# Norm scales from one product with ones, and shared landing buffers in the gate/up stage

## The chip, the cores and the metric

The kernel runs as one program on one core of a Trainium2 chip. A core has five engines, each with its own queue of instructions that it works off in order: TensorE (PE, matrix products; its weight loads are listed apart as PEld), VectorE (DVE), ScalarE (ACT), GpSimd (POOL) and SyncE (SP), which here only issues transfers. Engines wait for one another through semaphores. On-chip data lies in SBUF (128 partitions), products land in PSUM banks of 128 x 512 float32, and DMA engines move data between SBUF and device memory. The metric is the device time of one execution in microseconds. Three runs of the kernel before took 3178.4, 3183.67 and 3187.15 us; the median is 3183.67 us.

## The reference, cut to what matters

One layer of a decoder on 2048 positions of width 1024, in float32. The change touches the second norm, the gate/up and down products behind it, and the final norm:

```python
def rms_norm(x, g):
    y = xf * lax.rsqrt(jnp.mean(xf * xf, axis=-1, keepdims=True) + EPS)
    return (y * g).astype(x.dtype)

x = x + merged @ w_out
h = rms_norm(x, norm_ffn)
x = x + (jax.nn.silu(h @ w_gate) * (h @ w_up)) @ w_down
return rms_norm(x, final_norm)
```

`merged` is the gated sum of a sparse attention branch and a gMLP branch; both come earlier in the program and are not touched. D_FF is 2816.

## The kernel before

Activations are kept transposed: features on the partitions, positions along the free dimension, in tiles of 128 x 512. Every large product is made from three products of rounded parts: a float32 operand is split into a high part h (ACT copies it to the reduced type fp32r) and a low part l (DVE subtracts h), and PE sums h*h, h*l and l*h (`split` and `mm3`, lines 149 to 165). So each operand of each product needs an ACT copy and a DVE (or POOL) subtraction before PE can use it.

The program has stages one behind the other. The last three matter here.

**Output projection (1590 to 1883 us of the trace).** For each of four blocks `j` of 512 positions, the attention branch is projected and merged, eight tiles `m` of `merged @ w_out` are made into the PSUM tile `po`, x is added (`xo`), the result goes to device memory (`d_x1`, issued by ACT), and its squares are summed over `m` into `sq3`. When the next block reaches m = 1, `stats` (line 1055) makes the norm scales of the block that is done: PE takes the sums over partitions with four small products with a column of ones (`pss3`, one column for 128 positions), DVE copies four columns, ACT takes the root, DVE the reciprocal, and 512 scales `rr` are written to device memory as a row `d_rr`. `prep_b` (line 1020) then prepares the normed activations of half the positions (two blocks n) for two of the eight feature tiles (k and k + 4): per block it loads the row of scales back, spread over all partitions (`rbf`), loads two tiles of x (`x1s`), multiplies, and makes from the four tiles the seven right-hand operands of a Strassen product (`SB`; five are sums or differences, tile `cmb`, two are tiles as they are). They are written to device memory (`d_b`); in half 0 the operand for i = 1 is split at once and stays on chip. Half 0 is prepared in this stage (four calls, with blocks j = 2 and 3), half 1 in four calls after the pairs 2, 4, 6 and 8 of the gate/up stage.

**Gate/up (1883 to 2743 us).** The loops run over two halves of 1024 positions, eleven pairs `p` of feature tiles, seven Strassen products `i` in the order 1, 4, 5, 7, 3, 2, 6, and gate and up (g and u). Each of the 14 products of a pair has 12 matmuls of 512 columns into a bank `pgu`. Weights come in 1 MB transfers (`fraw`, three buffers); POOL forms their sums (`cmb`), ACT and DVE split them (`wfh`, `wfl`, six buffers each, so the splits run up to six products ahead). Products are copied by ACT and added by DVE into tiles `s`; at the pair's end `store_acts` makes silu(gate) * up, and DVE forms five sums and writes seven tiles to device memory (`d_a`). In pair 0 of half 0, `load_b` fetches the prepared operands one i at a time (`braw`) and splits them into `fh`, `fl`; pair 10 does the same for half 1. All short-lived tiles of this stage (`s`, `cmb` of DVE, `braw`, `rbf`, `x1s`) come from one set of 16 buffers, `tmp` (line 1158), opened when the output projection has closed its pools.

**Down (2743 to 3193 us).** Seven Strassen products over the pairs, with operands fetched from `d_a` and `d_w` and split again (`ua`, `uw`), PSUM tile `pdn`, sums `acc`. When a quarter is complete, `final` makes the final norm: four small products with ones, a DVE copy, root and reciprocal, then `bcast_rows` (line 134), which puts each scale on the diagonal of a 128 x 128 tile, in a high and a low part, and spreads it over the partitions with two products with `onesr`; ACT copies the result out of PSUM, DVE multiplies eight tiles, SP writes them to the output. This happens five times, three times for 512 positions and twice for 256; the last of them ends the program.

The order in which each engine works is not the order of the source. The program is built with a scheduler that simulates it and places each instruction where its model of the time finds room; a pool's buffers decide what can be placed early, since a tile can be written only when the tile that had its buffer is done with.

## Time and profile before

| what | value |
|---|---|
| median of three runs | 3183.67 us |
| the profiled execution, whole | 3195.09 us |
| its span, first to last instruction | 3193.0 us |
| mean granted TensorE clock | 0.978 of 2.4 GHz |
| busy share of the span | PE 96%, DVE 68%, ACT 45%, POOL 36% |
| PE busy, 1590 to 1883 us (output projection) | 278.3 of 293 us, clock 0.98 |
| PE busy, 1883 to 2743 us (gate/up) | 847.1 of 860 us, clock 0.99 |
| PE busy, 2743 to 3177 us (down) | 428.6 of 434 us, clock 1.00 |

The profiled execution is 11.4 us (0.4%) longer than the median run, so differences worked out from it are set against its own time and then carried over to the median. A busy share says how long an engine had an instruction in it. The granted clock says how much of the full 2.4 GHz TensorE was given: it has two levels, 1.2 and 2.4 GHz, so a stretch with a mean of 0.83 was in part at the lower one. A wait in the profile is put down to the engine or transfer whose signal came last.

### The profile page before, as it was taken

What the parts mean: (1) busy time and instruction counts of PE and PEld (TensorE: products, weight loads), DVE (VectorE), ACT (ScalarE), POOL (GpSimd) and SP (SyncE); (2) the same over time, 40 slices, a digit from 0 to 9 for tenths busy, and PEclk for the clock granted to TensorE, in tenths of its full rate; (3) what the DMA queues carried; (4) which work ended last, traced back from release to release, by engine and by line L of the source; (5) the groups of instructions that cost most, each with busy time, mean ns of one, the idle gap of its engine ahead of it and who ended that gap; (6) DMA issues with size and microseconds to landing.
All of it is one profiled execution on the core that took longest, in us unless ns stands there. A gap on an engine that the chain in (4) does not pass through costs nothing.

```text
span 3193.0 us, 43147 instructions
## 1 busy us (share of the span) xinstructions
PE 3057.4 (96%) x14550; PEld 2528.5 (79%) x14550; DVE 2162.7 (68%) x3846; ACT 1450.4 (45%) x2720; POOL 1163.4 (36%) x1186
## 2 busy tenths in 40 slices
PE   8799999999899999999899989999999999999998
PEld 7677888778688787888777778888878888788887
DVE  5648769869544787788643647777876777544565
ACT  6444554454234676677521134333443334333442
POOL 4453232343232323233353323333345555521220
PEclk9899999999899999999999999999999999999999
DMA  6533343333553222222465853444544444854453
GB/s 198 174 124 126 109 130 105 128 130 109 180 173 124 77 71 82 70 77 65 149 200 152 287 160 113 159 148 142 201 172 167 169 159 162 284 174 139 138 189 106
DMA packets 275681, 464.89 MB, mean 146 GB/s; under 512 B 41473, under 2 KB 99330, under 8 KB 275330
## 3 DMA queue, kind: packets, MB, share of 16 engines
q1 hardware_dynamic: 254146, 399.19, 39.3%
q0 software_dynamic: 16704, 54.54, 4.6%
q10 hardware_dynamic: 4608, 8.39, 0.7%
q8 instruction: 114, 1.87, 0.3%
q14 instruction: 109, 0.89, 0.1%
HBM read 307.93 MB, written 154.09 MB: 145 GB/s over the span
## 4 chain that ended last, share of the span: by engine, by line
PE 58%; DVE 6%; DMA 6%; ACT 2%; issue 2%; POOL 0%; SPq 0%; DVEq 0%; ACTq 0%; POOLq 0%
PE pgu L164 8%; PE pgu L163 8%; PE pgu L165 8%; PE pdn L164 4%; PE pdn L163 4%; PE pdn L165 4%; PE ptp L870 3%; DVE Pt L853 2%; PE O L877 2%; PE O L878 2%; PE ppr L163 1%; PE ppr L165 1%; PE ppr L164 1%; PE pg L165 1%; PE pg L163 1%
## 5 line engine op out<-in xcount | busy, mean ns | idle before, releaser
L1010 POOL TENSOR_TENSOR cmb<-fraw 128x512 f32<-128x512 f32 x275 | 401.5, 1465 | 487.4 <-DVE wfl L156 424.9
L163 PE MATMUL pgu<-fh,wfh 128*128 128x512 f32 x1232 | 480.2, 391 | 9.5 <-ACT fh L155 5.8
L164 PE MATMUL pgu<-fl,wfh 128*128 128x512 f32 x1232 | 481.9, 391 | 2.7 <-DVE fl L156 2.7
L165 PE MATMUL pgu<-fh,wfl 128*128 128x512 f32 x1232 | 481.5, 391 | 0.8 <-DVE wfl L156 0.7
L163 PEld LDWEIGHTS pgu<-fh,wfh 128*128 128x128 f32 x1232 | 232.4, 189 | 60.2 <-ACT fh L155 7.0
L164 PEld LDWEIGHTS pgu<-fl,wfh 128*128 128x128 f32 x1232 | 232.8, 189 | 52.4 <-DVE fl L156 4.0
L165 PEld LDWEIGHTS pgu<-fh,wfl 128*128 128x128 f32 x1232 | 232.7, 189 | 50.4 <-DVE wfl L156 2.4
L497 DVE SCALAR_TENSOR_TENSOR X<-rl,wi,X 128x512 f32<-128x512 f32 (+3 forms) x266 | 217.3, 820 | 78.6 <-ACT rl L493 63.1
L155 ACT ACTIVATE wfh<-cmb 128x512 fp32r<-128x512 f32 x220 | 138.5, 630 | 280.9 <-POOL cmb L1010 158.5
L156 DVE TENSOR_TENSOR wfl<-cmb,wfh 128x512 fp32r<-128x512 f32 x220 | 193.4, 886 | 101.2 <-ACT wfh L155 100.8
L164 PE MATMUL pdn<-ua,uw 128*128 128x512 f32 (+1 forms) x660 | 247.8, 376 | 3.9 <-DVE ua L156 3.9
L165 PE MATMUL pdn<-ua,uw 128*128 128x512 f32 (+1 forms) x660 | 245.9, 376 | 0.0
L163 PE MATMUL pdn<-ua,uw 128*128 128x512 f32 (+1 forms) x660 | 239.7, 376 | 1.5 <-ACT ua L155 1.5
L156 DVE TENSOR_TENSOR ua<-raw,ua 128x512 fp32r<-128x512 f32 (+1 forms) x165 | 121.0, 737 | 176.1 <-ACT ua L155 176.0
L1184 DVE TENSOR_TENSOR s<-s,pgu 128x512 f32<-128x512 f32 x264 | 174.7, 680 | 77.2 <-PE pgu L165 40.5
L163 PE MATMUL pm<-wh,hT 128*128 128x512 f32 (+1 forms) x576 | 218.7, 387 | 6.4 <-ACT wh L155 5.6
L164 PE MATMUL pm<-wl,hT 128*128 128x512 f32 (+1 forms) x576 | 219.5, 383 | 0.3 <-POOL wl L156 0.2
L155 ACT ACTIVATE pth<-ptp 128x512 fp32r<-128x512 f32 (+1 forms) x320 | 162.5, 532 | 123.9 <-PE ptp L870 114.6
L165 PE MATMUL pm<-wh,lT 128*128 128x512 f32 (+1 forms) x576 | 218.6, 381 | 0.0
L493 ACT ACTIVATE rl<-sc 128x512 f32<-128x512 f32 (+3 forms) x304 | 155.5, 547 | 133.2 <-PE sc L491 111.0
L163 PE MATMUL pg<-hT,wh 128*128 128x512 f32 x512 | 201.9, 394 | 8.0 <-ACT zg L458 8.0
L155 ACT ACTIVATE ua<-raw 128x512 fp32r<-128x512 f32 (+1 forms) x165 | 99.0, 602 | 242.4 <-PE pdn L165 204.2
(301 smaller groups left out, 7511.9 us busy)
## 6 DMA issues: line engine op xcount, KB each, us to landing
raw<-d_a SPq DMA_DIRECT2D x143, 256.0 KB, 2.7
wraw<-in_w_in_dram SPq DMA_DIRECT2D x64, 512.0 KB, 4.2
d_a<-cmb SPq DMA_DIRECT2D x110, 256.0 KB, 2.3
fraw<-in_w_gate_dram SPq DMA_DIRECT2D x22, 1024.0 KB, 5.1
fraw<-in_w_up_dram SPq DMA_DIRECT2D x22, 1024.0 KB, 6.8
d_sg<-zg POOLq DMA_DIRECT2D x64, 256.0 KB, 3.1
sg<-d_sg SPq DMA_DIRECT2D x64, 256.0 KB, 3.4
d_w<-cmb SPq DMA_DIRECT2D x55, 256.0 KB, 2.2
```

What stands on the lines that cost most here:

```text
L155: act.activation(h, src, AF.Copy)
L156: lo.tensor_tensor(l, src, _f(h), op=ALU.subtract)
L163: pe.matmul(out, ah, bh, start=first, stop=False, skip_group_check=onto)
L164: pe.matmul(out, ah, bl, start=False, stop=False, skip_group_check=onto)
L165: pe.matmul(out, al, bh, start=False, stop=last, skip_group_check=onto)
L493: act.activation(r[:, :w], sc[:, :w], AF.Relu)
L497: dve.scalar_tensor_tensor(xs, r[:, :w], wi[:, i, h:h + 1], xs, op0=ALU.mult, op1=ALU.add)
L853: dve.tensor_tensor_reduce(tiles[-1][0][:, po:po + w], sc[:, :w], masks[i][:, c0:c0 + w], -0.125, big if last is None else last, ALU.add, ...
L870: pe.transpose(pt[:, t * P:(t + 1) * P], out["P"][t, kt // 8][:, (kt % 8) * P:(kt % 8 + 1) * P], ident)
L877: pe.matmul(O[:, cs], V, a[:, cs], start=(kt == 0), stop=False)
L1010: eng.tensor_tensor(s, blocks[form[0]], blocks[form[1]], op=form[2])
L1184: dve.tensor_tensor(s[to], s[to], b, op=op)
```

## The change

The scales of both norms come from one product. `rms_rows` multiplies a 128 x 128 tile of ones with the tile of summed squares, in float32, so every partition holds the sum of every position; ACT takes the root from PSUM over the whole tile, and DVE the reciprocal of the whole tile. `stats` and `final` use it; `bcast_rows`, `onesr` and the row `d_rr` are gone. The scales of half 0 stay on chip in two buffers (`rbs`) until the last `prep_b` of half 0 has read them; those of half 1 are written as a full tile to `d_rb` and loaded from there.

The pool `pb` that held the short-lived tiles of `prep_b` in the output projection stays open through the gate/up stage: it has the two scale tiles and five buffers `pb3` instead of seven. `load_b`, `prep_b` of half 1 and the five sums of `store_acts` take these five buffers; only the sums of the very last pair take `tmp`, which has 12 buffers instead of 16.

```diff
--- before.py
+++ after.py
@@ -77,7 +77,7 @@
-    d_rr = tc.dram_tile([S], F32, name="d_rr")
+    d_rb = tc.dram_tile([P, S], F32, name="d_rb")
...
-    def bcast_rows(dst, cols, ntile, mk, tag):
-
-        for t0 in range(0, ntile, 4):
-            n = min(4, ntile - t0)
-            w = slice(0, n * P)
-            dh, dl = mk()
-            for t in range(n):
-                ts_, c = slice(t * P, (t + 1) * P), cols[:, t0 + t:t0 + t + 1]
-                dve.tensor_scalar(dh[:, ts_], ident, c, None, op0=ALU.mult)
-                dve.scalar_tensor_tensor(dl[:, ts_], ident, c, _f(dh[:, ts_]), op0=ALU.mult, op1=ALU.subtract)
-            pb = bank(tag, "pbc")
-            pe.matmul(pb[:, w], onesr, dh[:, w], start=True, stop=False)
-            pe.matmul(pb[:, w], onesr, dl[:, w], start=False, stop=True)
-            act.activation(dst[:, t0 * P:(t0 + n) * P], pb[:, w], AF.Copy)
+    def rms_rows(dst, sq, pb, sd):
+
+        pe.matmul(pb, ones, sq, start=True, stop=True)
+        act.activation(sd, pb, AF.Sqrt, bias=eps6, scale=1.0 / D)
+        dve.reciprocal(dst, sd)
...
-    pb_, _ = open_pool("pb", side="right", stack=c3)
+    pb_, _ = open_pool("pb", side="right", stack=c34)
...
-            rb = mk("rbf")
-            sp.dma_start(rb, d_rr[rows].partition_broadcast(P))
+            if half:
+                rb = mk("rbf")
+                sp.dma_start(rb, d_rb[:, rows])
+            else:
+                rb = rbs[n]
...
-        return pb_.tile([P, 512], dt, name=name, tag="pb3", bufs=7)
-
-    def stats(sa, rows, pl, tag="C"):
-
-        pss = bank(tag, "pss3")
-        for t in range(4):
-            pe.matmul(pss[:, t:t + 1], sa[:, t * P:(t + 1) * P], ones[:, 0:1], start=(t == 0), stop=(t == 3))
-        ss = pl.tile([P, 4], F32, name="ss3")
-        dve.tensor_copy(ss, pss[:, 0:4])
-        rr = pl.tile([P, 4], F32, name="rr3")
-        rstd(rr, ss, D, eps6, pl)
-        sp.dma_start(d_rr[rows].rearrange("(t p) -> p t", p=P), rr)
+        return pb_.tile([P, 512], dt, name=name, tag="pb3", bufs=5)
+
+    def stats(sa, rows, mk, tag="C"):
+
+        n = rows.start // 512
+        rb = pb_.tile([P, 512], F32, name="rb3", tag=f"rb{n}") if n < 2 else mk("rb3")
+        rms_rows(rb, sa, bank(tag, "pss3"), mk("sd3"))
+        if n < 2:
+            rbs[n] = rb
+        else:
+            sp.dma_start(d_rb[:, rows], rb)
...
-                stats(*after, pw)
+                stats(*after, sq3)
...
-        return fw.tile([P, 512], dt, name=name, tag="tmp", bufs=16)
+        return fw.tile([P, 512], dt, name=name, tag="tmp", bufs=12)
...
-            sp.dma_start(d_a[half, i, p], combine(SB[i], x, tmp, dve))
+            sp.dma_start(d_a[half, i, p], combine(SB[i], x, tmp if half and p == NP - 1 else pb3, dve))
...
-                    load_b(0, i, tmp)
+                    load_b(0, i, pb3)
...
-                    load_b(1, i, tmp)
+                    load_b(1, i, pb3)
             store_acts(half, p, *grp)
             if half == 0 and p == 0:
-                stats(*after, fw, "B")
+                stats(*after, tmp, "B")
             if half == 0 and p in (2, 4, 6, 8):
-                prep_b(1, p // 2 - 1, tmp)
+                prep_b(1, p // 2 - 1, pb3)
...
-        cs, nt = slice(c0, c0 + w), w // P
-        sa = sums[half, n][:, cs]
-        pss = bank("B", "pss4")
-        for t in range(nt):
-            pe.matmul(pss[:, t:t + 1], sa[:, t * P:(t + 1) * P], ones[:, 0:1], start=(t == 0), stop=(t == nt - 1))
-        ss = fy.tile([P, 4], F32, name="ss4")
-        dve.tensor_copy(ss[:, :nt], pss[:, :nt])
-        rr = fy.tile([P, 4], F32, name="rr4")
-        rstd(rr[:, :nt], ss[:, :nt], D, eps6, fy)
+        cs = slice(c0, c0 + w)
         rb = tmp5("rb4")
-        bcast_rows(rb, rr, nt, lambda: [tmp5("dgh", F32R), tmp5("dgl", F32R)], "B")
+        rms_rows(rb[:, :w], sums[half, n][:, cs], bank("B", "pss4")[:, :w], tmp5("sd4")[:, :w])
```

The scheduler orders the instructions anew from the output projection on; up to there every engine has the same order as before, but for one copy less at the start. Three places follow.

**ScalarE, start of the gate/up stage.** Before, from the last square of the output projection (`sal`); `wfh` is a weight split, `s` the copy of a finished product, `fh` the split of a normed operand:

```order
L1138 ACTIVATE sal<-xo 128x512
L1139 DMA d_x_100<-xo 128x512
L155 ACTIVATE wfh<-cmb 128x512
L1169 ACTIVATE s_20070<-pgu 128x512
L155 ACTIVATE wfh<-cmb 128x512
L1169 ACTIVATE s_20085<-pgu 128x512
L155 ACTIVATE fh<-braw 128x512 x4
L155 ACTIVATE wfh<-fraw 128x512
L1169 ACTIVATE s_20124<-pgu 128x512
L155 ACTIVATE wfh<-fraw 128x512
```

The same place now:

```order
L1129 ACTIVATE sal<-xo 128x512
L1130 DMA d_x_100<-xo 128x512
L144 ACTIVATE fh<-braw 128x512 x5
L144 ACTIVATE wfh<-cmb 128x512
L1160 ACTIVATE s_20034<-pgu 128x512
L144 ACTIVATE wfh<-cmb 128x512
L144 ACTIVATE fh<-braw 128x512
L1160 ACTIVATE s_20049<-pgu 128x512
L144 ACTIVATE fh<-braw 128x512 x5
L144 ACTIVATE wfh<-fraw 128x512
L1160 ACTIVATE s_20088<-pgu 128x512
```

The splits of the first operand (i = 4, four tiles) and one of i = 5 stood behind the copies of both products of i = 1; they now stand ahead of the first of them.

**SyncE's transfers, output projection, around the first scales.** Before (`ytk` are the tiles of the attention branch that the next block needs, `mb`, `sg`, `wpr`, `xo` other loads of the block):

```order
L921 DMA sg<-d_sg 128x512
L903 DMA ytk<-d_ya 128x4x128
L1101 DMA mb<-d_mb 128x512
L1064 DMA d_rr<-rr_18329 128x4x1
L903 DMA ytk<-d_ya 128x4x128
L921 DMA sg<-d_sg 128x512
L1029 DMA rbf<-d_rr 128x512
L1033 DMA x1s<-d_x_100 128x512
L1101 DMA mb<-d_mb 128x512
L1033 DMA x1s<-d_x_100 128x512
L903 DMA ytk<-d_ya 128x4x128
```

The corresponding place now:

```order
L1025 DMA x1s<-d_x_100 128x512
L1122 DMA xo<-in_xT_dram 128x512
L1092 DMA mb<-d_mb 128x512
L1122 DMA xo<-in_xT_dram 128x512
L1092 DMA mb<-d_mb 128x512
L1122 DMA xo<-in_xT_dram 128x512
L910 DMA sg<-d_sg 128x512
L892 DMA ytk<-d_ya 128x4x128
L1092 DMA mb<-d_mb 128x512
L892 DMA ytk<-d_ya 128x4x128
L910 DMA sg<-d_sg 128x512
L892 DMA ytk<-d_ya 128x4x128
```

The write of the scales and their load back are gone; this load of x (the other one stands seven rows further up) is now among the `xo` loads, ahead of the `ytk` loads.

**SyncE's transfers, half 0, behind pair 2 of gate/up (the first `prep_b` of half 1).** Before:

```order
L1029 DMA rbf<-d_rr 128x512
L1033 DMA x1s<-d_x_100 128x512 x2
L1041 DMA d_b_2_0_17407<-x1s 128x512
L1041 DMA d_b_5_0_17395<-x1s 128x512
L1041 DMA d_b_1_0_17387<-cmb 128x512
L1041 DMA d_b_4_0_17391<-cmb 128x512
L1041 DMA d_b_7_0_17399<-cmb 128x512
L1041 DMA d_b_3_0_17403<-cmb 128x512
L1041 DMA d_b_6_0_17411<-cmb 128x512
L1086 DMA fraw<-in_w_up_dram 128x2x1024
L1086 DMA fraw<-in_w_gate_dram 128x2x1024
```

Now:

```order
L1025 DMA x1s<-d_x_100 128x512 x2
L1019 DMA rbf<-d_rb 128x512
L1025 DMA x1s<-d_x_100 128x512
L1033 DMA d_b_2_0_17405<-x1s 128x512
L1025 DMA x1s<-d_x_100 128x512
L1033 DMA d_b_5_0_17393<-x1s 128x512
L1033 DMA d_b_1_0_17385<-cmb 128x512
L1077 DMA fraw<-in_w_up_dram 128x2x1024
L1033 DMA d_b_4_0_17389<-cmb 128x512
L1077 DMA fraw<-in_w_gate_dram 128x2x1024
L1033 DMA d_b_7_0_17397<-cmb 128x512
L1188 DMA d_a_2_3_17471<-s_21125 128x512
```

The five sums stood together ahead of the two weight loads (`fraw`); now two weight loads and a tile of the next pair (`d_a_2_3`) stand between them, since each sum needs a buffer that an earlier store has to free.

## Rows read from the trace of the kernel before

**Rows 1.** The page: span, TensorE's busy time, the chain's share by engine.

```profile
span 3193.0 us, 43147 instructions
...
PE 3057.4 (96%) x14550; PEld 2528.5 (79%) x14550; DVE 2162.7 (68%) x3846; ACT 1450.4 (45%) x2720; POOL 1163.4 (36%) x1186
...
PE 58%; DVE 6%; DMA 6%; ACT 2%; issue 2%; POOL 0%; SPq 0%; DVEq 0%; ACTq 0%; POOLq 0%
```

**Rows 2.** Windows: start:end, busy us (x instructions) per engine, clock, DMA share, GB/s.

```profile
1680.00:1700.00 20.00, 16.58 (x65) 12.77 (x64) 6.18 (x9) 2.35 (x4) 6.18 (x7) 0.91 0.80 207
1760.00:1800.00 40.00, 32.97 (x127) 25.62 (x126) 28.35 (x38) 8.08 (x14) 14.69 (x12) 0.87 0.97 315
1880.00:1920.00 40.00, 31.54 (x108) 23.65 (x107) 18.76 (x26) 15.41 (x29) 5.12 (x4) 0.83 0.48 165
1930.00:2300.00 370.00, 370.00 (x1638) 306.58 (x1637) 280.34 (x392) 155.20 (x269) 135.17 (x96) 1.00 0.43 149
2350.00:2370.00 20.00, 16.50 (x70) 12.47 (x69) 10.65 (x14) 5.58 (x10) 11.07 (x9) 1.00 0.32 114
```

**Rows 3.** Timeline of SyncE, 1747 to 1763 us: start, us, what it issued.

```profile
1747.37 0.37 SPq L1064 DMA_DIRECT2D d_rr<-rr  x1
...
1755.85 0.32 SPq L1029 DMA_DIRECT2D rbf<-d_rr  x1
...
1762.05 0.36 SPq L903 DMA_DIRECT2D ytk<-d_ya  x1
```

**Rows 4.** Waits, 1676 to 1702 us: us in total, times, longest.

```profile
DVE x1s L1034 <- DMA x1s<-d_x: 11.3, 1, 11.3
```

**Rows 5.** Waits, 1758 to 1774 us.

```profile
DVE x1s L1034 <- DMA x1s<-d_x: 11.7, 1, 11.7
...
PE pty L906 <- DMA ytk<-d_ya: 4.5, 1, 4.5
```

**Rows 6.** Timeline of ScalarE, 1884 to 1892 us.

```profile
1889.12 0.58 ACT L1169 ACTIVATE s<-pgu 128x512 f32<-128x512 f32 x1
1889.59 2.18 ACT L155 ACTIVATE fh<-braw 128x512 fp32r<-128x512 f32 x4
```

**Rows 7.** Waits of TensorE, 1880 to 1926 us.

```profile
PE pgu L163 <- ACT fh L155: 5.8, 3, 2.1
PE pgu L164 <- DVE fl L156: 2.7, 2, 1.8
```

**Rows 8.** Line 132, reciprocals: ns min/median/max, first and last start, forms.

```profile
L132 DVE RECIPROCAL rr<-sd x9: 165/178/178, 1674.6 to 3183.8; 128x4 f32<-128x4 f32 x7, 128x2 f32<-128x2 f32 x2
...
L132 DVE RECIPROCAL rk<-sd x1: 245/245/245, 154.4 to 154.4; 128x16 f32<-128x16 f32 x1
```

**Rows 9.** Timeline of TensorE, 3032 to 3033 us.

```profile
3032.30 0.94 PE L1290 MATMUL pss<-ones,sums 128*128 128x1 f32 x8
```

**Rows 10.** Timeline of VectorE, 2014 to 2034 us.

```profile
2014.73 0.69 DVE L1184 TENSOR_TENSOR s<-s,pgu 128x512 f32<-128x512 f32 x1 [1.43 <-PE pgu L165]
...
2016.66 4.07 DVE L1010 TENSOR_TENSOR cmb<-s,s 128x512 f32<-128x512 f32 x5
...
2030.55 3.10 DVE L1010 TENSOR_TENSOR cmb<-x1s 128x512 f32<-128x512 f32 x5
2033.57 0.69 DVE L156 TENSOR_TENSOR wfl<-cmb,wfh 128x512 fp32r<-128x512 f32 x1
```

**Rows 11.** Tile x1s, 1940 to 2300 us: its transfers, us from issue to landing.

```profile
DMA to landing us min/median/max: 2.0/5.4/6.9
```

**Rows 12.** The chain that ended last, from 3170 us: start, us, what.

```profile
3173.88 0.12 PE pdn L163
...
3182.20 1.03 PE pss L1290 x4
...
3185.66 0.39 ACT rb L147
3186.07 0.48 DVE acc L1300
```

More of the change, by code (lines that the diff above doesn't have):

```diff
@@ L104, in block_kernel @@
     ones = cp.tile([P, P], F32, name="ones")
-    onesr = cp.tile([P, P], F32R, name="onesr")
     eps6 = cp.tile([P, 1], F32, name="eps6")
@@ L119, in block_kernel @@
     dve.memset(ones, 1.0)
-    dve.tensor_copy(onesr, ones)
     dve.memset(eps6, 1e-6)
@@ L1011, in combine @@
         return s
-    fb, fbp = {}, {1: fb0}
+    fb, fbp, rbs = {}, {1: fb0}, {}
     def b_unit(half, i, k, src):
```

## The prediction

> **What bounds the kernel now.** I read the page's head first. TensorE is busy 3057.4 of 3193.0 us and heads the chain with 58% [rows 1]. So time is won only where TensorE stands, where it runs at the lower clock, or where its own work shrinks.
>
> Next I read busy time and granted clock in stretches of the two stages that the change touches [rows 2]. For each I add the idle time and the share that the clock lacks (1 minus granted clock, times the stretch); this sum I call the loss. 1930 to 2300 us, four and more pairs of gate/up, has none: 370.00 of 370.00 at 1.00. Three stretches lose:
> - 1680 to 1700: 20 − 16.58 = 3.4 idle, 0.09 × 20 = 1.8 clock, together 5.2.
> - 1760 to 1800: 40 − 32.97 = 7.0, 0.13 × 40 = 5.2, together 12.2.
> - 1880 to 1920: 40 − 31.54 = 8.5, 0.17 × 40 = 6.8, together 15.3.
>
> The first two lie in the output projection, behind its norm scales; the third is the start of gate/up. The views of waits and the timelines of these stretches then say what ends last there.
>
> In the output projection SyncE works in order. It issues the write of the scales at 1747.37 and the load that reads them back, `rbf`, only at 1755.85, 8.5 us later; behind that stands the next `ytk`, issued at 1762.05 [rows 3]. The transfers of x behind it come late: VectorE stands 11.7 us at its first `x1s`, with the `mgl` and `sg` work of the next block queued behind, and TensorE waits 4.5 us for `ytk` [rows 5]. The block before shows the same: VectorE stands 11.3 us at `x1s` [rows 4].
>
> At the start of gate/up, ScalarE copies a product at 1889.12 and only then makes the four `fh` splits, 1889.59 to 1891.77 [rows 6]. TensorE waits for such splits: 5.8 us in three waits for `fh`, 2.7 us in two for `fl` [rows 7]. It stands, the clock drops, and it needs longer for what comes next.
>
> **The change, part by part.**
>
> *Scales of half 0 kept on chip.* The write of `d_rr`, the load of `rbf` and the 8.5 us between them go, and the x loads stand before them. What is late next: prep_b holds four tiles of x in five buffers, so its last two sums each wait for the landing of an earlier store, and VectorE will stand there some 2 to 3 us at a time (a landing of x takes 2.0 to 6.9 us, median 5.4 [rows 11]). `mgl` and `sg` are queued behind VectorE's sums as they were behind `x1s`. So not all of 5.2 + 12.2 = 17.4 comes back; bounds 0 and −17.4, I take −10, as one stand of 11 us is replaced by some of 2 to 3.
>
> *Landing buffers open before gate/up begins.* Before, `tmp` opened only when the output projection had closed. Now the five `braw` tiles can land earlier, and ScalarE has five splits ahead of the first copy. Two of the three waits for `fh` thereby lose their cause, and most of the clock loss with them. What is late next: the other 23 loads go through five buffers, one freed at each subtraction; the operand of i = 5 has about one microsecond of margin in the order. Bounds: −15.3 (all of it) and −5 (only the first wait of about 2 and its share of the clock); I take −12.
>
> *TensorE's own work.* A 512-column sum with one column per 128 positions took 0.94 us [rows 9]. Four such in the stats and three in the final norms go (6.6 us), two half-sized ones (0.9), and the spreading products: three times two of 512 columns, at 370/1638 = 0.226 us a matmul [rows 2], 1.4 us, and twice two of 256 at 0.12 [rows 12], 0.5 us. Removed 9.4 us. Added: seven float32 products of 512 columns and two of 256, or eight of 512. None is in the trace. The small float32 products left two records each (eight records for four [rows 9]); if a record costs what a matmul of 512 columns costs here, a product costs 0.45 us, and if it costs double, 0.91. Added 3.6 to 7.3 us, net −6 to −2; I take −3, nearer the dear end, since one-column products at 0.94/8 = 0.12 us a record show nothing cheap.
>
> The Trainium skill, "FP8 and Floating Point Precision", TensorE Precision Notes, says that true FP32 takes four passes through the array; by that a 512-column product would cost 0.9 us and this term would be −2 rather than −3. The trace of before has no float32 product of this width to compare with, only the two records for each small one.
>
> *Reciprocals.* These were 128x4 at 178 ns and one 128x16 at 245 [rows 8]: (245 − 178)/12 = 5.6 ns a column, so 128x512 comes to 178 + 508 × 5.6 = 3.0 us and 128x256 to 1.6. Of the nine, four stand in the output projection and the first pair, where VectorE has idle time (28.35 busy of 40 us even at 1760 to 1800, 280.34 of 370 in gate/up [rows 2]), four in the down stage under products, where each also replaces small VectorE work (a copy and the diagonal tiles), and one in the tail, below. Cost 0 while VectorE is not late. Uncovered, two of them would add 6 us to the output projection; the bound 0 of the first term holds that.
>
> *The tail.* Only the last final norm is bare. Before: from 3182.20 (sums) to 3186.07 (first product with the scales), 3.9 us [rows 12]. After: one float32 product of 256 columns (0.5), root 0.4, reciprocal 1.6, and some 0.8 for the handovers between four engines' steps (an estimate: the old 3.9 less its 1.03 and 0.39 [rows 12] is 2.5 us for a copy, a reciprocal of 0.17, the diagonals, two products and all their handovers): 3.3 us. Term −0.6, bounds −1.5 and +0.7.
>
> The Trainium skill, "VectorE: DVE Perf Modes", First, the fixed hardware budget, says that the reciprocal runs an iterative divide with a repeat count of 8. If that multiplied the 0.69 us of a plain 128x512 operation, it would take 5.5 us, 2.8 for half, and the tail would be +0.6. The slope of the two rows speaks for the shorter one.
>
> *Prep_b of half 1, through five buffers.* Before, VectorE makes the five sums of the pair from 2014.73 and 2016.66 on, five of prep_b by 2033.65, and the split of the next weight at 2033.57 + 0.69 = 2034.3 [rows 10]. TensorE needs that weight ten products behind 2014.7: 2014.7 + 10 × 12 × 0.226 = 2041.9. Slack 7.6 us. Now the fourth x tile is loaded only after a buffer is free, and each sum waits for the landing of an earlier one's store, with those stores behind 1 MB weight loads in SyncE's queue. What waits behind VectorE's sums is the weight splits, and TensorE behind them. I estimate two microseconds more, within the slack: cost 0 per pair. Pair 10 loads 28 tiles through five buffers instead of up to sixteen, and 2350 to 2370 already lacks 20 − 16.50 = 3.5 us [rows 2]: +2 for it, bounds 0 and +8.
>
> *Last pair's sums, `tmp` with twelve buffers, and the change of stage to down:* no row prices them; nearest is that 1930 to 2300 stands nowhere with sixteen. I take 0, bounds ±1.
>
> Sum: −10 − 12 − 3 − 0.6 + 2 = −23.6 us. Against the profiled execution, 3195.1, that is 3171.5; the median run is 11.4 below it, so 3160. The bounds of the terms, all good or all bad, are −17.4 − 15.3 − 6 − 1.5 − 1 = −41 and 0 − 5 − 2 + 0.7 + 8 + 1 = +3.
>
> **The rivals.**
>
> *One of the two stretches pays.* Either VectorE's stands in half 0's prep_b take the place of that for x1s, or the loads behind the first five come too late and TensorE stands on `braw` instead of `fh`. For it: five buffers for four x tiles and seven results; against it, five splits stand in front. −10 to −12, less the products' 3, plus 2 to 5: about −10, 3174.
>
> *All gain given back.* Both happen and pair 10 loses its eight: −5 − 2 + 0.7 + 5 = about −1, 3182.
>
> *Slower: the five sums become serial.* In each of pairs 2, 4, 6 and 8, store_acts writes five sums and prep_b five more and loads four tiles, all through five buffers, each of which comes free only when a store has landed. If a round of store, landing and next sum takes 5.4 us at the median landing [rows 11], and three rounds a pair lie bare, 16 us, the split of the next weight is late by 16 − 7.6 = 8 to 10 us, and TensorE stands that long and starts again at the lower clock. Four times 10 is +40, against −22: +18, 3202. It decides from the point where the waits of a pair pass 7.6 + 22/4 = 13 us. Against it: VectorE has 90 of 370 us free, the stores are issued while splits are interleaved, and 1930 to 2300 has no loss to begin with.
>
> **How the numbers follow.** What this kernel can tell from no change is about 0.3%, 9.5 us, so under 3174.1 is faster. The forecast, 3160, has 0.58, with a range of its own from 3150 to 3172; one stretch only 0.20, about half of it under 3174; all given back 0.09; serial sums 0.13. Faster is 0.57 + 0.09 = 0.66, same 0.11 + 0.08 + 0.01 = 0.20, slower 0.14. The range goes from 3146 (nearly all of the two stretches comes back) to 3181 (one stretch pays and pair 10 loses); above lie the serial case and part of the third, below little, some 0.2 in all.
>
> **What would show it.** Right, if after 1880 us the first `fh` split ends before the first copy of a product, TensorE has no wait over 1 us for `fh`, and the 40 us stretch at the start of gate/up is busy at 1.00 or nearly; if VectorE's wait for `x1s` is under 3 us at the first two prep_b, with no TensorE wait on `ytk`; if a float32 product of 512 columns shows 0.45 to 0.91 us, a 128x512 reciprocal 3.0, and 3.3 us lie between the last sums and the first product with scales. Prep_b's sums in pairs 2, 4, 6 and 8 should show VectorE waiting on landings a few microseconds with TensorE at 1.00 busy beside it. Wrong, if TensorE stands for `wfl` in the pair after any of these four, if waits on `braw` take the place of those on `fh`, or if a stretch of 1690 to 1880 loses as much as before with VectorE standing at `cmb` for a store.

## The result and the profile after

The changed kernel took 3161.75 us (median of six runs, 3153.05 to 3166.72) against 3185.49 for the kernel before beside it: ratio 0.9922, 95% interval 0.9908 to 0.9936, some 20 to 29 us. On another chip the same pair gave 0.9941 (0.9928 to 0.9954), 20.8 us between the medians. The forecast was 3160, by −23.6 us; the medians of the first chip differ by 23.7.

The profiled executions differ by more, 33.2 us of span. The stages tell why. The columns below are worked out from the first start of the `po`, `pgu` and `pdn` products and the last start of `pdn` in each trace:

| us | up to first `po` | output projection | gate/up | down | tail |
|---|---|---|---|---|---|
| before | 1599.6 | 283.5 | 861.0 | 433.7 | 15.2 |
| after | 1594.0 | 273.3 | 847.5 | 431.4 | 13.6 |
| difference | −5.6 | −10.2 | −13.5 | −2.3 | −1.6 |

The first column is work that the change does not touch; in the fourteen traces of this study it lies between 1594.0 and 1602.5. The other four differ by 27.6 us. Of these the down stage spreads by itself (431.4 to 436.0 in traces with the new final norm as it is, 433.7 and 436.4 in the two with the old), and so does the tail (15.2 and 12.9 with the old code), so −2.3 and −1.6 tell little. The output projection and gate/up carry the result, 23.7 us together.

The page of the kernel after, which answers to [rows 1]:

```profile
span 3159.8 us, 42892 instructions
...
PE 3040.8 (96%) x14494; PEld 2515.8 (80%) x14494; DVE 2186.8 (69%) x3804; ACT 1452.5 (46%) x2715; POOL 1166.0 (37%) x1186
```

TensorE's busy time fell by 16.6 us; part of it is products that are gone and part is products that no longer ran at the lower clock (mean granted clock 0.978 before, 0.982 after). Windows of the kernel after (start:end, length, then busy time with instructions for PE, PEld, DVE, ACT, POOL, granted clock, DMA share, GB/s), shifted to the same work as in [rows 2], with two stretches that are new:

```profile
1674.00:1694.00 20.00, 20.00 (x96) 16.66 (x95) 11.31 (x15) 4.71 (x8) 11.56 (x10) 1.00 0.73 228
1750.00:1790.00 40.00, 38.56 (x173) 31.08 (x172) 28.37 (x39) 7.57 (x13) 12.93 (x11) 1.00 0.91 292
1800.00:1820.00 20.00, 15.26 (x56) 11.43 (x55) 17.32 (x21) 4.34 (x7) 10.04 (x8) 0.83 0.71 233
1864.00:1904.00 40.00, 39.91 (x177) 32.72 (x176) 33.80 (x45) 26.74 (x47) 13.30 (x8) 1.00 0.57 195
1910.00:2250.00 340.00, 340.00 (x1502) 281.53 (x1501) 258.02 (x348) 137.19 (x236) 130.58 (x90) 1.00 0.41 146
2260.00:2320.00 60.00, 56.68 (x239) 46.33 (x238) 55.45 (x76) 37.00 (x67) 24.58 (x16) 0.94 0.66 229
```

The three losses of before (5.2, 12.2 and 15.3 us) are 0, 1.4 and 0.1. A new one stands at 1800 to 1820: 4.7 idle and 0.17 × 20 = 3.4 of clock, 8.1 us. At 2260 to 2320 another 3.3 + 0.06 × 60 = 6.9 are lost. Waits of the kernel after, 1800 to 1870 us, name the new one (engine, line, what ended the wait: us in total, times, longest):

```profile
DVE x1s L1026 <- DMA x1s<-d_x: 6.2, 2, 5.7
...
PE pss L134 <- DVE sq L1132: 4.7, 1, 4.7
```

The float32 product of block 2's sums stands in TensorE's queue before VectorE has made the sums; VectorE itself had stood 5.7 us at a load of x.

Where gate/up gained and lost can be worked out from the starts of the `pgu` products, 168 of them in a pair. A pair takes 38.1 us where nothing waits. The first pair of half 0 took 55.3 us before and takes 38.9 now. Pair 10 takes 38.1 in both kernels. The first pair of half 1, right behind it, took 40.7 and takes 44.4, and the first three of half 1 together 120.2 and 122.6. So the 6.9 us lost at 2260 to 2320 lie in the first pair of half 1, which begins at 2287.5. There TensorE waits for an addition of VectorE, which has the splits of the last `braw` tiles in between (waits of the kernel after, 1920 to 2300 us; the first line is for half 1's preparation, which comes up at the end):

```profile
DVE x1s L1026 <- DMA x1s<-d_x: 19.6, 9, 2.9
...
PE pgu L152 <- DVE s L1175: 3.3, 1, 3.3
```

The start of gate/up, ScalarE's timeline of the kernel after (start, us, engine, line, what), answers to [rows 6]:

```profile
1868.81 2.70 ACT L144 ACTIVATE fh<-braw 128x512 fp32r<-128x512 f32 x5
1871.42 0.61 ACT L144 ACTIVATE wfh<-cmb 128x512 fp32r<-128x512 f32 x1
1871.93 0.57 ACT L1160 ACTIVATE s<-pgu 128x512 f32<-128x512 f32 x1
```

Five splits, then the first copy. TensorE has no wait for `fh` or `fl` there.

The new operations, line 134's product and line 136's reciprocal in the kernel after (ns min/median/max, first and last start, shapes):

```profile
L134 PE MATMUL pss<-sq,ones x6: 590/591/1191, 1668.0 to 1810.4; 128*128 128x512 f32 x6
...
L136 DVE RECIPROCAL rb<-sd x9: 1753/3352/3353, 1669.8 to 3151.0; 128x512 f32<-128x512 f32 x7, 128x256 f32<-128x256 f32 x2
```

Six records are three products, two each. How long TensorE is held by one is read from the starts of its neighbours:

```profile
1668.02 1.02 PE L134 MATMUL pss<-sq,ones 128*128 128x512 f32 x2
1668.47 0.80 PE L154 MATMUL ppr<-yth,wpl 128*128 128x512 f32 x1
1669.11 0.40 PE L152 MATMUL ppr<-yth,wph 128*128 128x512 f32 x1
```

From 1668.02 to 1669.11 lie the product and one ordinary matmul of 0.23: the product takes 0.86 us. The reciprocal takes 3.35 us for 512 columns and 1.75 for 256, 6.2 ns a column. The end of the chain, after (start, us, what), answers to [rows 12]:

```profile
3149.22 1.24 PE pss L134 x2
3150.48 0.48 ACT sd L135
3150.98 1.76 DVE rb L136
3152.77 0.48 DVE acc L1283
```

From the sums' product to the first product with scales it is 3.55 us, before 3.87. A second trace of each norm (the buffers alone, below, has the old one) has 3.03 and 3.46.

### The profile page after: what moved, and what is told of

The parts are those of the page before. It is cut to its first block, busy times and chain, and to the rows that moved or that the text cites. A ratio compares the mean times of both kernels' runs of the same rounds, so it can differ in the third digit from the quotient of the medians.

```text
span 3159.8 us, 42892 instructions
## 1 busy us (share of the span) xinstructions
PE 3040.8 (96%) x14494; PEld 2515.8 (80%) x14494; DVE 2186.8 (69%) x3804; ACT 1452.5 (46%) x2715; POOL 1166.0 (37%) x1186
## 4 chain that ended last, share of the span: by engine, by line
PE 57%; DVE 6%; DMA 5%; issue 2%; ACT 2%; POOL 1%; SPq 0%; DVEq 0%; ACTq 0%; POOLq 0%
PE pgu L153 7%; PE pgu L152 7%; PE pgu L154 7%; PE pdn L152 4%; PE pdn L153 4%; PE pdn L154 4%; PE ptp L859 3%; PE O L866 2%; PE O L867 2%; DVE Pt L842 2%; PE ppr L152 1%; PE ppr L153 1%; PE ppr L154 1%; PE pg L154 1%; PE po L152 1%
## 5 line engine op out<-in xcount | busy, mean ns | idle before, releaser
L145 DVE TENSOR_TENSOR wfl<-cmb,wfh 128x512 fp32r<-128x512 f32 x220 | 180.8, 830 | 73.2 <-ACT wfh L144 72.8
```

The source lines that it names most:

```text
L145: lo.tensor_tensor(l, src, _f(h), op=ALU.subtract)
```

## The experiments

Each ratio is to the kernel before, run beside it on the same chip. The changed kernel itself gave 0.9922 and 0.9941 on two chips, so ratios that differ by 0.002 tell little; the stages of the traces are read first. Those of the changed kernel's second trace are 273.0 for the output projection, 847.3 for gate/up and 433.7 for down.

**The scales alone, and the buffers alone.** The first keeps the new scales and closes `pb` as before (`load_b`, `prep_b` of half 1 and `store_acts` use `tmp` again):

```diff
-    pb_, _ = open_pool("pb", side="right", stack=c34)
+    pb_, _ = open_pool("pb", side="right", stack=c3)
-        return fw.tile([P, 512], dt, name=name, tag="tmp", bufs=12)
+        return fw.tile([P, 512], dt, name=name, tag="tmp", bufs=16)
```

> The new scales alone (on-chip rows of scales, one float32 product), with all short-lived tiles of gate/up back in the 16 buffers of tmp. Theory A (two separate gains: the scales pay in the output projection, the landing buffers at the start of gate/up): output projection, first po to first pgu, about 273 us as in the changed kernel (before 283.5); gate/up, first pgu to first pdn, about 860 (before 861.0, changed 847.5); whole -10 - 3 of products = about -13 us, ratio 0.996. Rival B (the buffers alone pay, the scales save only products): output projection 281 or more, ratio 0.999. TensorE waits for fh at the start of gate/up as before, 5 us or more in total.

Measured: ratio 0.9947 (0.9933 to 0.9962); output projection 272.9, gate/up 858.0. The second is the kernel before with the reverse of these lines (and seven `pb3`).

> The pool change alone: scales through device memory and four small products as before, with seven landing buffers (two scale tiles' room is free) kept open through gate/up, tmp 12. Theory A: output projection about 283, as before, VectorE standing some 10 us at x1s twice; gate/up about 848; ratio 0.996. Rival B: gain in both stages, ratio 0.993 or less. Rival C (the new order pays only as a whole): no gain, ratio 0.999 to 1.001.

Measured: ratio 0.9935 (0.9920 to 0.9951); output projection 286.3, gate/up 845.6. The two gains are separate: each edit gains 10 us or more in its own stage and moves the other's by 3 us at most. The ratios are both better than the 0.996 of theory A, and taken together (0.53% and 0.65%) they are more than the 0.6 to 0.8% of the whole change, so the shares are read from the stages. The 40 us from the start of gate/up, first the scales alone, then the buffers alone:

```profile
1874.00:1914.00 40.00, 31.54 (x107) 23.62 (x106) 20.22 (x29) 17.03 (x32) 5.11 (x4) 0.83 0.48 164
```

```profile
1887.00:1927.00 40.00, 40.00 (x182) 33.26 (x181) 36.80 (x53) 28.16 (x51) 12.13 (x8) 1.00 0.53 177
```

The first is [rows 2] at 1880 to 1920 over again, the second has no loss.

**Which tiles in the buffers matter.** The changed kernel, with only the first operands back in `tmp`:

```diff
-                    load_b(0, i, pb3)
+                    load_b(0, i, tmp)
```

> The changed kernel, but the operands that gate/up loads first (braw, pair 0) land in tmp, which opens only when the output projection has closed. Theory A (the gain at the start of gate/up is the early landing): gate/up gives back some 12 us, to about 859, TensorE waits for fh again, ratio to before 0.996. Rival D (the gain in gate/up comes from the smaller tmp and the other tiles in the landing buffers): gate/up stays at 848 to 850, ratio 0.992 to 0.993.

Measured: ratio 0.9973 (0.9962 to 0.9985); gate/up 865.9, output projection 273.4. The early landing of `braw` is the gain in gate/up. TensorE's waits in this run, 1864 to 1930 us, are those of [rows 7] again, with a little more for `fl`:

```profile
PE pgu L152 <- ACT fh L144: 5.7, 3, 2.1
...
PE pgu L153 <- DVE fl L145: 4.1, 3, 1.8
```

It gives back 18 us and not 12, nearly all in the first pair (57.0 us, 38.9 in the changed kernel). Against the kernel before it is 5 us longer: 1.7 in the first pair, 2.8 in the first of half 1, and the rest in pairs of half 1 further on. `tmp` has twelve buffers here and had sixteen there; whether that is the cause was not tried.

**Half 0's scales through device memory.**

```diff
-            if half:
+            if True:
                 rb = mk("rbf")
                 sp.dma_start(rb, d_rb[:, rows])
...
-        rb = pb_.tile([P, 512], F32, name="rb3", tag=f"rb{n}") if n < 2 else mk("rb3")
+        rb = mk("rb3")
...
+        sp.dma_start(d_rb[:, rows], rb)
```

> The changed kernel, but the scales of half 0 too are written to device memory as a full tile and loaded back by every prep_b; seven landing buffers, since the two scale tiles are not needed. Theory A (the round trip through SyncE's queue costs the time): output projection back to 280 to 284, VectorE waiting 8 us or more at x1s or rbf twice, gate/up about 848, ratio 0.995 to 0.996. Rival E (the small products and the new reciprocal's place made the difference, not the round trip): output projection 273 to 276, ratio 0.992 to 0.993.

Measured: ratio 0.9905 (0.9887 to 0.9924); output projection 274.2, gate/up 846.0. Theory A fell: the write and the load back are there, and the time is not. (The run has seven landing buffers; a sixth alone, below, leaves the output projection at 273.0.) SyncE's timeline of this run shows what is different:

```profile
1744.84 0.32 SPq L1052 DMA_DIRECT2D d_rb<-rb  x1
1746.36 0.43 SPq L892 DMA_DIRECT2D ytk<-d_ya  x1
1747.26 0.32 SPq L1019 DMA_DIRECT2D rbf<-d_rb  x1
```

The load goes out 2.4 us behind the write, in [rows 3] 8.5 us. Before, the write was 512 numbers of four bytes, each to its own address (`(t p) -> p t`); here it is 128 rows of 2 KB, 128 times as many bytes. In the kernel before, SyncE's own waits, 1740 to 1770 us, say what stood in front of the load, and the tile `d_rr`, 1747 to 1748 us, when the write landed; the third line is the write of whole rows, tile `d_rb` of this run, 1679 to 1682 us:

```profile
SPq L1029 <- DMA d_rr<-rr: 7.5, 1, 7.5
...
DMA to landing us min/median/max: 8.5/8.5/8.5
...
DMA to landing us min/median/max: 2.8/2.8/2.8
```

The write issued at 1747.37 landed 8.5 us later, to the tenth the gap in front of the load, and for 7.5 of these SyncE waits for it. Another write of this form has its landing in the same trace, 9.7 us; the four of whole rows took 2.4 to 6.0.

**A slow write put back.** The run above, with one of the 128 rows written as before was, and the other 127 by a write of their own:

```diff
-        sp.dma_start(d_rb[:, rows], rb)
+        if n < 2:
+            sp.dma_start(d_rb[1:, rows], rb[1:])
+            sp.dma_start(d_rb[0, rows].rearrange("(t p) -> p t", p=P), rb[:, 0:4])
+        else:
+            sp.dma_start(d_rb[:, rows], rb)
```

> The run with half 0's scales through device memory, but row 0 of the scales is written as 512 pieces of four bytes, as the row of before was (127 rows as whole pieces; the values of that row are those of the first four columns, so the output of one feature in 128 is wrong). Theory F (what cost the time before was the slow landing of that scattered write, 5.7 to 9.7 us against 2.4, for which SyncE stands ahead of its next loads): the gap from the write's issue to the load of the scales grows from 2.9 to 6 to 9 us twice, output projection from 274.2 to 280 to 284, whole 6 to 10 us above the run with whole rows (about 3170, ratio 0.994). Rival E (the small products and their VectorE steps were the cause, not the write): output projection 273 to 276, ratio 0.991.

Measured: ratio 0.9995 (0.9984 to 1.0006); output projection 295.6, gate/up 844.7. SyncE's timeline of this run:

```profile
1750.89 4.08 SPq L1054 DMA_DIRECT2D d_rb<-rb  x1
1755.02 2.40 SPq L892 DMA_DIRECT2D ytk<-d_ya  x1
...
1763.95 0.33 SPq L1019 DMA_DIRECT2D rbf<-d_rb  x1
1764.40 1.21 SPq L892 DMA_DIRECT2D ytk<-d_ya  x2
```

and TensorE's waits in it, 1640 to 1880 us:

```profile
PE pty L895 <- issue: 8.7, 1, 8.7
PE pty L895 <- DMA ytk<-d_ya: 6.2, 1, 6.2
```

The gaps are 12.8 and 13.1 us, and the stage 21.4 us longer than with whole rows, both more than theory F expected. But the run is no clean test of it, since it has a second slow write, which the edit made by the way: the 127 other rows. The packets of the trace show them one behind the other, 2 KB every 0.08 us, from 1751.4 to 1762.3, while the 128 rows of the run before went out side by side in about 1 us. Windows as above, this run first, then the write of whole rows in the run before:

```profile
1751.00:1755.00 4.00, 4.00 (x22) 3.29 (x21) 2.84 (x4) 0.83 (x2) 3.69 (x4) 1.00 0.08 19
```

```profile
1745.40:1746.40 1.00, 1.00 (x6) 0.84 (x5) 0.56 (x1) 0.00 (x0) 0.91 (x1) 1.00 0.69 260
```

Most of the 512 small pieces went out at 1755.5 to 1757, some 30 only at 1762.9, when the rows were done, and the landing followed at 1763.9. In between, three issues took SyncE 4.1, 2.4 and 2.4 us (0.37 for the write of before), and only 4.0 of the 13.1 us are a wait for the landing. The load of `mb` issued there took 9.9 us to land. TensorE's second wait is for `ytk`, queued behind, as in [rows 5]; for the first the profile names no releaser, and VectorE stands 12.0 us at `x1s` there (11.3 in [rows 4]).

So the run shows what a slow write in front of that load does to the stage, and not what the scattered write of the kernel before cost. For that write there is its own trace: 8.5 and 9.7 us to land, 7.5 us of waiting by SyncE against 0.4 with whole rows. The kernel before with this one write in whole rows was not run; how much of the 10 us is the write's, and how much is left for rival E, stays open. The Trainium skill, "DMA: Bandwidth & Descriptors", Why small descriptors are slow (HBM only), says that each packet and each descriptor of a transfer carries a fixed cost whatever its size. The trace of the kernel before agrees in that 2 KB in 512 pieces took longer to land than 256 KB in 128 rows (8.5 and 2.8 us), but the cost of moving the pieces does not fill the time: they went out at 1748.3 to 1748.6, other loads ran up to 1751, and from there to the landing the DMA engines are idle. What ends the time is open. The window of the kernel before:

```profile
1751.00:1755.80 4.80, 4.80 (x23) 3.92 (x22) 0.78 (x1) 0.00 (x0) 3.17 (x3) 1.00 0.00 0
```

**Block 2's scales behind pair 0.** They are not needed before pair 2:

```diff
-            if after and m == 1:
+            if after and j < 3 and m == 1:
                 stats(*after, sq3)
...
             if half == 0 and p == 0:
+                stats(*late, tmp, "B")
                 stats(*after, tmp, "B")
```

> The changed kernel, but the scales of block 2 are made with those of block 3 behind pair 0 of gate/up (its summed squares stay in a tile of their own). In the changed kernel TensorE stands 4.7 us at 1804.6 to 1809.3 for the sum that this product needs, and 1800 to 1820 us loses 8.1 us with the clock. Theory A: output projection 273.3 minus 5 to 8, about 267; gate/up +1 (one product more, 0.85 us); ratio to before 0.989 to 0.990. Rival: TensorE stands at the next thing that VectorE owes it (mgl) instead, output projection 271 to 274, ratio 0.992.

Measured: ratio 0.9920 (0.9906 to 0.9933); output projection 272.2. The wait is gone and another of 4.5 us stands there; the rival holds:

```profile
PE ppr L152 <- DVE sg L911: 4.5, 1, 4.5
```

**Six landing buffers** (`bufs=6` for `pb3`).

> The changed kernel with six landing buffers instead of five. The terms of the prediction for five buffers: half 0's sums waiting for a store (VectorE 6.8 us in four waits at cmb), pair 10's 28 loads (1.9 + 1.2 + 3.3 = 6 us lost between 2260 and 2320). If the buffers set them: VectorE's waits at cmb for stores in the output projection go to 3 us or less, loss at 2260 to 2320 halves, whole -2 to -4 us, ratio 0.991. If not: ratio 0.992 and the same loss.

Measured: ratio 0.9920 (0.9906 to 0.9933); output projection 273.0, gate/up 844.8. VectorE's waits for a store fell, and TensorE at 2280 to 2300 is busy 19.08 of 20 (the first pair of half 1 takes 39.9 us, not 44.4). So gate/up is 2.7 us shorter; the ratio of the whole does not show it. VectorE's waits up to the end of the output projection, first the changed kernel, then this run:

```profile
DVE cmb L999 <- DMA d_b<-cmb: 6.8, 4, 2.8
```

```profile
DVE cmb L999 <- DMA d_b<-cmb: 2.3, 1, 2.3
```

**Reciprocals three times over.**

```diff
         dve.reciprocal(dst, sd)
+        dve.reciprocal(sd, dst)
+        dve.reciprocal(dst, sd)
```

> The changed kernel with two reciprocals more behind each of the nine (value, its inverse, the value again): the step that the change made dearest, 3.35 us of VectorE for 512 columns, three times over. Prediction's term (reciprocals cost nothing where VectorE is not late, and 1.75 us bare in the tail): output projection 273 to 275, gate/up 847 to 849, tail 13.6 + 3.5 = 17, whole about +4 us, ratio 0.993 to 0.994. Rival (VectorE is the late engine behind the scales, as TensorE's stand of 4.7 us for the sum at 1804 to 1809 suggests): output projection 279 to 285, the 6.7 us more per scales showing as TensorE's waits, ratio 0.996 or more.

Measured: ratio 1.0009 (0.9998 to 1.0021); output projection 280.0, gate/up 846.0, down 446.8, tail 24.2. The rival holds. The tail's 10.6 us more are 3.5 of its own two further reciprocals and 7.1 of a longer wait for the sums in front of it, since the set before it holds VectorE too. TensorE's waits of this run, 2980 us to its end, and the same of the changed kernel:

```profile
PE pss L134 <- DVE sums L1275: 9.8, 1, 9.8
PE pdn L155 <- DVE ua L147: 7.4, 4, 5.5
PE pdn L154 <- DVE acc L1316: 1.6, 1, 1.6
```

```profile
PE pss L134 <- DVE sums L1273: 2.7, 1, 2.7
PE pdn L153 <- DVE ua L145: 1.4, 1, 1.4
```

**A faster version: VectorE's pile spread.**

```diff
-            if (j, m) in ((2, 1), (2, 4), (2, 6), (3, 0)):
-                prep_b(0, {(2, 1): 0, (2, 4): 1, (2, 6): 2, (3, 0): 3}[j, m], pb3, keep=(1,))
+            if (j, m) in ((2, 1), (2, 4), (3, 0), (3, 3)):
+                prep_b(0, {(2, 1): 0, (2, 4): 1, (3, 0): 2, (3, 3): 3}[j, m], pb3, keep=(1,))
...
-        return pb_.tile([P, 512], dt, name=name, tag="pb3", bufs=5)
+        return pb_.tile([P, 512], dt, name=name, tag="pb3", bufs=6)
```

> A try for a faster version: six landing buffers, and the third and fourth preparation of half 0 later (at blocks and tiles (3, 0) and (3, 3) instead of (2, 6) and (3, 0)), so that VectorE's work behind the scales does not pile up before 1810 us. If VectorE's pile is what TensorE stands for there: no stand for the sum, output projection 266 to 270, ratio 0.989 to 0.990. If the scheduler's order or other waits set it: 272 to 274, ratio 0.992.

Measured: ratio 0.9894 (0.9875 to 0.9913); output projection 268.7. TensorE still waits 0.9 us for the sums. It was run again beside the changed kernel:

> The changed kernel once more, beside the spread version on the same chip: ratio to before 0.992.

> The spread version once more: if its gain over the changed kernel is there (output projection 268.7 against 273.3 us, no stand of TensorE for the sum), ratio to before 0.989 to 0.990 and a median 6 to 10 us under the changed kernel's on the same chip; if the first time was luck of the runs, within 3 us of it.

Measured: the changed kernel 3168.03, 0.9941 (0.9928 to 0.9954); the spread version 3160.03, 0.9916 (0.9903 to 0.9929), output projection 269.9. So it is 8 us faster than the changed kernel on that chip, as expected, though both ratios came out 0.002 above the expected ones. The trace has 3.1 us of this in the output projection and 2.2 in gate/up (845.1), where the sixth buffer alone had as much; later preparation without the sixth buffer was not run. In this run TensorE has no wait for the sums, and the stretch that lost 8.1 us is full:

```profile
1800.00:1820.00 20.00, 20.00 (x88) 16.19 (x87) 16.07 (x18) 5.59 (x9) 13.97 (x12) 1.00 0.90 295
```

**The spread version without reciprocals.**

```diff
-        act.activation(sd, pb, AF.Sqrt, bias=eps6, scale=1.0 / D)
-        dve.reciprocal(dst, sd)
+        act.activation(sd, pb, AF.Ln, bias=eps6, scale=1.0 / D)
+        act.activation(dst, sd, AF.Exp, scale=-0.5)
```

> The spread version with the scales as exp(-0.5 ln(mean + eps)) on ScalarE, so that VectorE makes no reciprocal (3.35 us for 512 columns, nine times). Tripled reciprocals cost 6.7 us in the output projection, 15 in the down stage and 10.6 in the tail. If one reciprocal costs in the same measure: output projection -2 to -3 (266), down and tail -3 to -6, whole 4 to 8 us under the spread version, ratio 0.987 to 0.988. If single reciprocals still fit beside the products: tail alone -1 to -1.8, ratio the same as the spread version within 0.001; loading ScalarE's tables for the other functions may take that back.

Measured: ratio 0.9935 (0.9920 to 0.9951); output projection 268.5, down 440.3, tail 13.0. ScalarE's timeline near the end of this run:

```profile
3152.86 1.28 ACT L135 ACT_TABLE_LOAD   x1
3155.05 0.47 ACT L135 ACTIVATE sd<-pss,eps 128x256 f32<-128x256 f32 x1 [0.91 <-PE pss L134]
3155.54 1.28 ACT L136 ACT_TABLE_LOAD   x1
3156.84 0.42 ACT L136 ACTIVATE rb<-sd 128x256 f32<-128x256 f32 x1
```

Neither forecast came: the run is 6.7 us slower than the spread version beside it. Each function has a table of its own to load, 1.28 us, two loads for every set of scales (18 in all, 3 in the spread version); the second stands in the path where the reciprocal stood. The output projection is 1.4 us shorter, the tail the same (13.2 there), and the down stage 6 us longer (434.3 there), with TensorE's waits for `ua` up from 3.9 to 6.8 us; that the tables are its cause was not tried apart.

## Why the prediction was right, and where its reasons were not

The sum held: −23.6 forecast, −23.7 in the medians, and −23.7 in the output projection and gate/up of the two traces. That it came within 0.1 us is luck: the interval is 20 to 29 us, the second chip gave 20.8, and the landing buffers gave more than their term.

*Scales on chip, −10: right size, wrong reason.* The stage gave −10.2, and −10.6 with the scales alone. The step that failed is "the write of `d_rr`, the load of `rbf` and the 8.5 us between them go" as the thing that pays by its going. The chain from there on was right: SyncE stands in order, `ytk` and x come late, VectorE stands at x and TensorE waits. But with the round trip kept and its write in whole rows the stage takes 274.2 us, and with a write that lands after 13 us it takes 295.6. What filled the 8.5 us was the landing of one write of four-byte pieces; that this write made the stage's 10 us is argued from the waits, and not shown by a run that changes it alone. The prediction read the length of the gap from [rows 3] and did not ask what filled it; the landing time of `d_rr` was in the same trace. It also took the `ytk` of 1762.05 for the next one; [rows 3] leaves out two that were issued before it, behind the same load, and TensorE's wait ends at 1765.8, when the first of these has landed (SyncE's timeline of the kernel before):

```profile
1759.02 1.08 SPq L903 DMA_DIRECT2D ytk<-d_ya  x2
```

*Landing buffers, −12: right in kind, too small.* Early landing of `braw` alone decides it. The loss fell to 0.1 us, 15.2 less, the whole of the bound, rather than by 12; the first pair is 16.4 us shorter. The loads behind the first five (19, not the prediction's 23: six operands of four tiles) came in time: ScalarE waited for `braw` six times, 1.1 us at most.

*TensorE's work, −3: right.* Seven products of 0.86 us and two of half that (taken, not read) are 6.9 us against the 9.4 that the prediction removes, −2.5. Read from their neighbours' starts, as the new product is, the old four held TensorE 0.90 us and not 0.94, which makes it −2.2. The Trainium skill's four passes for true FP32 ("FP8 and Floating Point Precision", TensorE Precision Notes) gave an estimate of 0.9 us and −2; the trace agrees with the price.

*Reciprocals, 3.0 us and cost 0: size nearly right, cost in doubt.* 3.35 us were measured. The Trainium skill's repeat count ("VectorE: DVE Perf Modes", First, the fixed hardware budget), taken as a multiplier, gave 5.5; the trace does not bear that reading out. But VectorE is late behind the scales: 6.7 us more per set lengthen the output projection by 6.7 us and the down stage by 13 to 15. What single reciprocals cost remains unmeasured, since the run without them put the work on ScalarE.

*What is late next.* The prediction named VectorE's stands at sums that wait for stores. They were there, 6.8 us in four, and with a sixth buffer they fell without a gain in the output projection. What TensorE really waited for was the new product of sums at 1809 us, an 8.1 us loss in the changed kernel that the prediction did not have. Taking that product away only moved the stand to the next thing that VectorE owes. With the preparation spread and a sixth buffer it went, and the stage came to 268.7 and 269.9; so VectorE's pile in front of the last sums is its cause as far as these runs show.

*The tail, −0.6:* −0.3 and −0.4 from the sums on (3.87 to 3.55, 3.46 to 3.03).

*Prep_b of half 1 through five buffers, 0, and the slower rival:* right. VectorE waits for x nine times there, 2.9 us at most, and 1910 to 2250 us is 340.00 of 340.00 at 1.00. The slack covers it.

*Pair 10, +2: right size, wrong place.* The prediction took the 3.5 us lost at 2350 to 2370 for pair 10. They lie in half 1, whose first pair begins at 2319.2, and TensorE waits there for the split of a weight; pair 10 itself loses nothing, before or after. What the five buffers cost stands in the first pair of half 1, 3.7 us, or 2.4 over the first three (2.1 and 0.9 in the changed kernel's second trace). With six buffers the first pair takes 39.9 to 41.1. (In the rival of all gain given back, the sum takes 5 us where the text says eight; with eight it comes to some +2.)

## What to carry to other kernels

When an in-order queue stands between a write and the load that depends on it, read the write's own landing time and the size of its pieces before taking the trip away: 512 pieces of four bytes took 8.5 and 9.7 us to land here, 256 KB in rows 2.4 to 6.0. When you put a cost back to test it, look in the trace that it came back in the same form: here the write of the 127 other rows was the slower one. At a change of stage, ask which pool opens too late for the first loads of the next one; five buffers that are open early took 16 us out of the first pair here, more than the new norm took out of its stage. And when one edit frees a queue, look which engine's work has piled up behind it: spreading it, with a sixth buffer, was worth another 8 us on one chip.

## What the runs showed of the hardware that was not expected

A write of 512 four-byte pieces (128 x 4 numbers) took 8.5 and 9.7 us to land, though its pieces went out in about 0.4 us; 256 KB in 128 rows of 2 KB took 2.4 to 6.0. A write of 127 such rows went out row by row in 10.9 us, where 128 rows took about 1. Why is not shown by these runs. A float32 product of 512 columns held TensorE 0.86 us, in two records; a reciprocal of 512 columns held VectorE 3.35 us.
